# Holding the weights instead of the tokens in the input GEMMs of three FFNs and a convolution mixer

## The chip, the cores and the metric

The kernel runs on one core of a Trainium2 chip. The metric is the device time of one execution in microseconds (us). Three runs of the kernel before gave a median of 1300.48 us, from 1299.72 to 1302.66. The core has five engines that run side by side, each through its own instructions in a fixed order: TensorE (PE, matrix products; its weight loads are listed apart as PEld), VectorE (DVE), ScalarE (ACT), GpSimd (POOL) and SyncE (SP), which here issues all transfers. TensorE multiplies a stationary operand of up to 128 x 128, loaded beforehand, with a moving operand of up to 512 columns and adds the product into a PSUM bank of 128 partitions x 512 fp32 words. There are eight banks. SBUF is the working memory of 128 partitions.

## What is computed

Two layers of a diffusion backbone with 256 latent and 256 context tokens, width 1024, in fp32. Layer 0 is a half-step SwiGLU FFN (latent and context), neighbourhood attention, and a second FFN; layer 1 is an FFN, a gated short convolution, and an FFN. Each sub-layer ends in a residual and a LayerNorm. Cut to what matters:

```
def swiglu_ffn(h, w_in, w_out):                 # w_in (1024, 2*2816), w_out (2816, 1024)
    a, u = jnp.split(h @ w_in, 2, axis=-1)
    return (jax.nn.silu(a) * u) @ w_out

def half_step_ffn(x, shift, scale, gate, w_in, w_out, g, b):
    y = swiglu_ffn(modulate(x, shift, scale), w_in, w_out)      # x * (1 + scale) + shift
    return post_norm_update(x, y, gate, 0.5, g, b)              # layer_norm(alpha*x + 0.5*gate*y)

def short_conv_mixer(h, w_in, conv_w, w_out):   # w_in (1024, 3072)
    b_gate, c_gate, hv = jnp.split(h @ w_in, 3, axis=-1)
    u = c_gate * hv
    y = conv_w[0]*up[:, 0:n] + conv_w[1]*up[:, 1:n+1] + conv_w[2]*up[:, 2:n+2]   # up: u padded by one token
    return (b_gate * y) @ w_out
```

The modulation vectors (shift, scale, gate) are products of a conditioning vector with 18 matrices of 1024 x 1024.

## The kernel before

**Precision.** Every operand of a large product is split exactly into a high part (hi) that the matmul's fast fp32 format holds and the rest (lo); a product is hi*hi + hi*lo + lo*hi, three matmuls. The high part is a ScalarE copy, the low part a VectorE subtraction (`split`, L104 to L106). Weights come by DMA into a raw tile, 256 rows of 512 columns at a time (a *unit*, `wunit` L162), and are split by two ScalarE copies (L178) and two VectorE subtractions (L181). There are 4 raw, 5 hi and 5 lo tiles, and up to three more pairs in some stages, so units are prepared ahead of their use.

**The input GEMMs.** `panels` (L361) goes through the columns of w_in in *panels* of 512: 256 columns of `a` and the matching 256 of `u`. A panel has four units, and there are two tiles of 128 latent tokens, t = 0 and 1. For each (tile, panel, unit), a *chunk*, `mmu` (L152) issues six matmuls with the tokens stationary (128 rows of the width x 128 tokens) and the weights moving (512 columns): L156, L157 for hi*hi and hi*lo, L159 for lo*hi. The first two panels run in an order (`lead_in`) that lets the first token tile start before the second is ready; from the third on, the two tiles alternate unit by unit. A bank holds 128 tokens x 512 columns. When it is full, `done` in `gated` (L380) takes SiLU of its first half on ScalarE (L386) and multiplies by its second half on VectorE (L387). Four chunks later TensorE transposes the result (L395, four transposes of 128 x 128 for both tiles of a panel) into a bank with the 256 columns on the partitions and the tokens along the row, which is then split (L105, L106, named gh and gl): that is the stationary operand of the output GEMM. An FFN has 11 panels. The convolution's input GEMM has 6: two for the gate b, which are transposed by themselves, and four for the products c * hv, which take the same path with a copy in place of SiLU; `conv` then works on the transposed product.

The first FFN of layer 0 is written apart (`f0_mm`, L533): there the weights are stationary and 512 tokens, latent and context, move.

**The tokens.** `modulated` (L324) takes a normalized token tile, transposes it in two halves, applies scale and shift on ScalarE (L341) and splits it into hTh and hTl, tiles of 128 x 512 each, from a pool of 38 such tiles (`act`) that also holds x, the split gated products, gate rows and LayerNorm rows.

**Order.** TensorE's order is the order of the code. The instructions of the other engines are ordered by a planner from modelled times and priorities: `tc.high_priority(offset=n)` moves what it encloses n places ahead. Weights go 40 places ahead, the LayerNorm's and the tokens' work 60 (`LN_EARLY`). The next layer's modulation vectors are made in the background (`ada`, L228): their matrices come by DMA, VectorE sums them up (L242, L244, named acc), and a few matmuls (L260) add over the partitions; a step of it is issued for about every third chunk, 20 places late. PSUM's eight banks are three named mm, three named at and two named tp; token tile 0 uses mm, token tile 1 at, the transposes tp.

Of the kernel before, what the change touches and what calls it, by code (L numbers as in the profile page):

```python
# [28 lines left out]
NACT = 38  # L29
# [35 lines left out]
def backbone_kernel(  # L65
# [28 lines left out]

    def bank(tag, s):
        return pp.tile([P, 512], F32, tag=tag, bufs=PB[tag], name=nm(s))
# [16 lines left out]
    class Late:  # L113
        """work whose TensorE part goes behind n more chunks, or to where its result is first asked for"""
# [37 lines left out]
    def mmu(ps, ops, first, last):  # L152
        """ops: [(lh, ll, rh, rl)] of one unit: hi*hi + hi*lo + lo*hi"""
# [8 lines left out]
    def wunit(srcs, kn, s):  # L162
        """srcs: [(source [P, kn, m], first column)]; returns the exact split (hi, lo), each [P, kn, 512]."""
# [119 lines left out]
    def fold_cols(l, v, m, ln):  # L283
        """column tiles [P, 8] of G = g*(1+scale) and B = b*(1+scale)+shift."""
# [38 lines left out]

    def modulated(z, mv, rs, GB, lag):  # L324
        """z <- norm; -> Late list over halves of (hi, lo) [128 d, 4 chunks, 128 tok] of norm*G + B."""
# [3 lines left out]
        def rest():  # L329
            G, B = GB.get()  # L330
            res = []
            for h in range(2):
# [4 lines left out]
                with tc.high_priority(offset=LN_EARLY):  # L337
                    hi, lo = act(F32R, "hTh"), act(F32R, "hTl")
# [3 lines left out]
                    split(t, hi, lo)  # L342
# [3 lines left out]
        return Late(lag, rest)  # L346

    def hsl(hT, k):
        hi, lo = hT.get()[k // 4]
        s = (k % 4) * P  # L350
        return hi[:, s:s + P], lo[:, s:s + P]

# [1 line left out]
    def lead_in(np):  # L354
        """(tile, panel, unit): the first tile is ready before the second."""
# [3 lines left out]
        return o + [(t, p, u) for p in range(2, np) for u in r for t in range(2)]  # L359

    def panels(cols, w, hTs, order, done, s):  # L361
# [14 lines left out]
    def run(gen):  # L376
        for _ in gen:
            pass
# [682 lines left out]
```

## Time and profile before

| | |
|---|---|
| median of 3 runs | 1300.48 us (1299.72 to 1302.66) |
| profiled execution, first to last instruction | 1296.6 us |
| granted TensorE clock, mean | 0.995 |
| TensorE busy | 1259.6 us (97%), 5890 matmuls |
| weight loads busy | 1006.5 us (78%), 5890 loads |
| VectorE busy | 956.2 us (74%) |
| ScalarE busy | 588.3 us (45%) |
| DMA | 274.92 MB, mean 212 GB/s |

The profiled execution has no other time than this span; the runs' times, taken without the profiler, lie a few microseconds above it. In the profile L12 is line 12 of the kernel; `w1h<-w1r` is what an instruction writes and reads, by the program's tile names; `128x512` is partitions x elements. Behind the bar of a group stand its busy time in us, the mean of one in ns, and the engine's idle time just before, with what ended it. A row of the timeline is start, duration, engine, line, instruction, and in brackets the idle time before it. Matmuls overlap: a row's duration is from a matmul's start to its modelled end, and the time that one takes of TensorE is the distance to the next one's start. Stages by their matmuls: first FFN and attention to 612 us; second FFN's input GEMM 612 to 744 and output GEMM to 809; third FFN's 811 to 939 and to 1003; convolution's input GEMM 1003 to 1074 and output to 1099; fourth FFN's 1100 to 1228 and to 1289.

### The profile page before, as it was taken

How to read it: one execution, taken by the hardware profiler on the slowest of the kernel's cores; microseconds unless marked ns; L12 is line 12 of the kernel's file. 1: busy time of each engine (PE TensorE's matmuls, PEld its weight loads, DVE VectorE, ACT ScalarE, POOL GpSimd, SP SyncE). 2: the span in 40 equal slices, each digit the busy share in tenths (PEclk: the TensorE clock that was granted, in tenths of full speed). 3: DMA queues.
4: the chain of work that ended last, by engine and by line, in shares of the span. 5: the costliest groups of instructions: out<-in, count | busy, mean ns of one | idle time of the engine just before them, and what ended most of it. 6: DMA issues, size and time to landing. Idle time of an engine off the chain costs nothing.

```text
span 1296.6 us, 17135 instructions
## 1 busy us (share of the span) xinstructions
PE 1259.6 (97%) x5890; PEld 1006.5 (78%) x5890; DVE 956.2 (74%) x1691; ACT 588.3 (45%) x1148; POOL 14.4 (1%) x37
## 2 busy tenths in 40 slices
PE   7999989999999999998999999999999999999997
PEld 4787767878778878766787787787788877788886
DVE  3698678686648867788997888767878788865545
ACT  2433013331324556587654534654535644655431
POOL 0000000000001000000000000000000000000000
PEclk9999989999999999999999999999999999999999
DMA  9877578867431632353997988666887664675641
GB/s 283 283 238 237 158 228 277 262 217 246 150 130 53 205 125 74 106 155 101 313 330 257 322 326 302 212 211 209 294 300 255 204 220 148 205 225 179 219 163 57
DMA packets 200305, 274.92 MB, mean 212 GB/s; under 512 B 21196, under 2 KB 145588, under 8 KB 200218
## 3 DMA queue, kind: packets, MB, share of 16 engines
q1 hardware_dynamic: 200218, 273.83, 64.7%
q8 instruction: 46, 0.75, 0.2%
q14 instruction: 41, 0.34, 0.1%
HBM read 269.77 MB, written 4.01 MB: 211 GB/s over the span
## 4 chain that ended last, share of the span: by engine, by line
PE 73%; DMA 12%; DVE 7%; ACT 3%; issue 2%; SPq 1%; POOL 0%; DVEq 0%; ACTq 0%
PE w L156 12%; PE w L157 12%; PE w L159 12%; PE f L538 6%; PE f L539 6%; PE f L540 5%; DMA ar<-in_ada_w_dram 4%; DMA braw<-in_na_rpb_dram 4%; DMA w1r<-in_ffn_w_in_dram 4%; PE wkv L156 2%; PE wkv L157 2%; PE wkv L159 2%; DVE w1l L181 2%; DVE acc L244 2%; PE wc L156 2%
## 5 line engine op out<-in xcount | busy, mean ns | idle before, releaser
L178 ACT ACTIVATE w1h<-w1r 128x512 fp32r<-128x512 f32 x352 | 202.4, 626 | 210.9 <-DMA w1r<-in_ffn_w_in_dram 105.0
L181 DVE TENSOR_TENSOR w1l<-w1r,w1h 128x512 fp32r<-128x512 f32 x352 | 227.3, 686 | 60.4 <-ACT w1h L178 58.0
L156 PE MATMUL w<-w1h,hTh 128*128 128x512 f32 x528 | 210.8, 399 | 4.0 <-ACT hTh L105 4.0
L244 DVE SCALAR_TENSOR_TENSOR acc<-ar,cst,acc 128x512 f32<-128x512 f32 x266 | 187.9, 747 | 34.6 <-DMA ar<-in_ada_w_dram 34.4
L157 PE MATMUL w<-w1l,hTh 128*128 128x512 f32 x528 | 207.0, 392 | 0.0
L156 PE MATMUL w<-w2h,gh 128*128 128x512 f32 (+1 forms) x446 | 175.4, 394 | 0.0
L157 PE MATMUL w<-w2l,gh 128*128 128x512 f32 (+1 forms) x446 | 173.5, 390 | 1.0 <-DVE w2l L181 1.0
L178 ACT ACTIVATE w2h<-w2r 128x512 fp32r<-128x512 f32 x176 | 101.5, 624 | 144.4 <-PE w L159 126.0
L159 PE MATMUL w<-w1h,hTl 128*128 128x512 f32 x528 | 163.4, 391 | 0.6 <-DVE hTl L106 0.6
L181 DVE TENSOR_TENSOR w2l<-w2r,w2h 128x512 fp32r<-128x512 f32 x176 | 113.9, 686 | 44.6 <-ACT w2h L178 44.0
L539 PE MATMUL f<-h0h,w1l 128*128 128x512 f32 x352 | 139.2, 395 | 4.6 <-DVE w1l L181 4.6
L538 PE MATMUL f<-h0h,w1h 128*128 128x512 f32 x352 | 140.5, 399 | 0.0
L540 PE MATMUL f<-h0l,w1h 128*128 128x512 f32 x352 | 139.0, 395 | 0.0
L159 PE MATMUL w<-w2h,gl 128*128 128x512 f32 (+1 forms) x446 | 136.5, 387 | 0.0
L156 PEld LDWEIGHTS w<-w1h,hTh 128*128 128x128 f32 x528 | 99.2, 188 | 28.0 <-ACT hTh L105 5.3
L159 PEld LDWEIGHTS w<-w1h,hTl 128*128 128x128 f32 x528 | 99.0, 188 | 23.9 <-DVE hTl L106 1.5
L157 PEld LDWEIGHTS w<-w1l,hTh 128*128 128x128 f32 x528 | 99.2, 188 | 20.4 <-DVE w1l L181 0.3
L156 PEld LDWEIGHTS w<-w2h,gh 128*128 128x128 f32 x446 | 83.7, 188 | 21.7 <-issue 1.7
L157 PEld LDWEIGHTS w<-w2l,gh 128*128 128x128 f32 x446 | 83.7, 188 | 18.8 <-DVE w2l L181 1.4
L159 PEld LDWEIGHTS w<-w2h,gl 128*128 128x128 f32 x446 | 83.3, 188 | 19.0 <-DVE gl L106 0.3
L539 PEld LDWEIGHTS f<-h0h,w1l 128*128 128x128 f32 x352 | 67.1, 191 | 19.0 <-DVE w1l L181 5.0
L538 PEld LDWEIGHTS f<-h0h,w1h 128*128 128x128 f32 x352 | 66.9, 190 | 18.0 <-issue 4.1
(176 smaller groups left out, 1677.7 us busy)
## 6 DMA issues: line engine op xcount, KB each, us to landing
w1r<-in_ffn_w_in_dram SPq DMA_DIRECT2D x352, 256.0 KB
ar<-in_ada_w_dram SPq DMA_DIRECT2D x128, 512.0 KB
w2r<-in_ffn_w_out_dram SPq DMA_DIRECT2D x88, 512.0 KB
ar<-in_ada_w_dram SPq DMA_DIRECT2D x32, 256.0 KB
wkvr<-in_na_w_qkv_dram SPq DMA_DIRECT2D x32, 256.0 KB
wcr<-in_sc_w_in_dram SPq DMA_DIRECT2D x32, 256.0 KB
wqr<-in_na_w_qkv_dram SPq DMA_DIRECT2D x8, 512.0 KB
bias<-bscr SPq DMA_DIRECT2D x64, 64.0 KB
```

The costliest lines, as they stand in the source:

```text
L156: nc.tensor.matmul(ps, lh, rh, start=first and i == 0, stop=False)
L157: nc.tensor.matmul(ps, lh, rl, start=False, stop=False)
L159: nc.tensor.matmul(ps, ll, rh, start=False, stop=last and i == n - 1)
L178: nc.scalar.activation(hi[:, a:a + m // W_HI], raw[:, a:a + m // W_HI], AF.Copy)
L181: nc.vector.tensor_tensor(out=lo[:, a:b], in0=raw[:, a:b], in1=hi[:, a:b].bitcast(F32), op=ALU.subtract)
L244: nc.vector.scalar_tensor_tensor(out=a, in0=src, scalar=sc, in1=a, op0=ALU.mult, op1=ALU.add)
L538: nc.tensor.matmul(ps, lh, hT0[k][0], start=(k == 0), stop=False)
L539: nc.tensor.matmul(ps, ll, hT0[k][0], start=False, stop=False)
L540: nc.tensor.matmul(ps, lh, hT0[k][1], start=False, stop=(k == KC - 1))
```

## The change

From the third panel on, the input GEMMs of the second, third and fourth FFN and the four product panels of the convolution hold the weights and move the tokens. For this the modulated latent tokens are written into two tiles `hx` of 128 x 4 x 512, one for each half of the width: for each of four 128-row chunks, the hi parts of all 256 tokens and beside them the lo parts. `modulated` writes its hi and lo there instead of into tiles of the pool, which has 30 tiles in place of 38; the two `hx` tiles take as many bytes as the eight left out. (The first FFN's tokens, and those of the attention, use `hx` too, with the same instructions as before.)

A panel is now worked unit by unit for both token tiles at once. For each of two column blocks j of 128 and for z = a, u, `direct_unit` loads 128 x 128 of the hi weights and moves hi and lo of the tokens side by side (512 columns into a whole bank), then loads the lo weights and moves the hi tokens (256 columns into the bank's first half). In the panel's last unit the lo weights come first. A panel fills four banks at a time, two mm and two at, each with 128 columns of the weights on the partitions; the two halves of a bank have still to be added. When a column block's two banks are full, `direct` copies the second half out on ScalarE, adds the first half on VectorE, for a and for u, and then takes SiLU (ScalarE) and the product (VectorE). After the second column block the result is split as before. There are no transposes, since the columns stand on the partitions already, and no delay of four chunks. All of it is issued 60 places ahead. The number of steps between which background work is issued is the same.

```
-NACT = 38
+NACT = 30
+    def hx_tile():
+        return ap.tile([P, 4, 512], F32R, tag="hx", bufs=2, name=nm("hx"))
...
-                    hi, lo = act(F32R, "hTh"), act(F32R, "hTl")
+                    if hx is None:
+                        hi, lo = (act(F32R, n).rearrange("p (k c) -> p k c", k=4) for n in ("hTh", "hTl"))
+                    else:
+                        if len(hx) <= h:
+                            hx.append(hx_tile())
+                        hi, lo = (hx[h][:, :, v * 256 + c0:v * 256 + c0 + P] for v in range(2))
...
-        return o + [(t, p, u) for p in range(2, np) for u in r for t in range(2)]
+        return o + [(None, p, u) for p in range(2, np) for u in r]
...
+    def direct_unit(banks, unit, u, hTs):
+        hi, lo = unit
+        hx = hTs[0].hx
+        for t in range(2):
+            hTs[t].get()
+        for j in range(2):
+            for z in range(2):
+                ps = banks[2 * j + z]
+                c = slice(z * 256 + j * P, z * 256 + (j + 1) * P)
+                for i in range(UK):
+                    k = UK * u + i
+                    h = hx[k // 4][:, k % 4]
+                    last = u == KU - 1
+                    for part in ((1, 0) if last else (0, 1)):
+                        w, m = ((hi, 512), (lo, 256))[part]
+                        nc.tensor.matmul(ps[:, 0:m], w[:, i, c], h[:, 0:m], start=(u == i == part == 0),
+                                         stop=(last and i == UK - 1 and part == 0))
+            yield j
...
+            if t is None:
+                if u == 0:
+                    banks[p] = [mmb(s, z) for _ in range(2) for z in range(2)]
+                for j in direct_unit(banks[p], units[p, u], u, hTs):
+                    if u == KU - 1:
+                        direct(p, j, *banks[p][2 * j:2 * j + 2])
+                    yield
+                    tick()
+                continue
...
+        def direct(p, j, a, u):
+            if j == 0:
+                gs[p] = sp.tile([P, 512], F32, tag="s2", bufs=S2, name=nm("sil"))
+            g = gs[p][:, j * 256:(j + 1) * 256]
+            with tc.high_priority(offset=LN_EARLY):
+                t = sp.tile([P, 512], F32, tag="tmp", bufs=3, name=nm("au"))
+                for z, bk in enumerate((a, u)):
+                    c = slice(z * 256, (z + 1) * 256)
+                    nc.scalar.activation(t[:, c], bk[:, 256:512], AF.Copy)
+                    nc.vector.tensor_tensor(out=t[:, c], in0=bk[:, 0:256], in1=t[:, c], op=ALU.add)
+                nc.scalar.activation(g, t[:, 0:256], func)
+                nc.vector.tensor_tensor(out=g, in0=g, in1=t[:, 256:512], op=ALU.mult)
+                if j == 1:
+                    res.append(finish(p, gs.pop(p)))
...
-            hi, lo = act(F32R, "h0h"), act(F32R, "h0l")
+            hi, lo = (z[:, k] for z in hx0) if k < 4 else (act(F32R, "h0h"), act(F32R, "h0l"))
...
-                hTs[t] = modulated(xt[t], mv, rs, GB[t // 2], F0_LAG[t])
+                hTs[t] = modulated(xt[t], mv, rs, GB[t // 2], F0_LAG[t], hx1 if t < 2 else None, t % 2 * P)
```

More of the change, by code (lines that the diff above doesn't have):

```diff
@@ L322, in finish_stats, with modulated @@
         return mv, rs
-    def modulated(z, mv, rs, GB, lag):
+    def modulated(z, mv, rs, GB, lag, hx=None, c0=0):
         for h in range(2):
@@ L341, in rest @@
                         nc.scalar.activation(t[:, s], ps[:, s], AF.Identity, bias=B[:, c], scale=G[:, c])
-                    split(t, hi, lo)
+                    split(t.rearrange("p (k c) -> p k c", k=4), hi, lo)
                 res.append((hi, lo))
             return res
-        return Late(lag, rest)
+        late = Late(lag, rest)
+        late.hx = hx
+        return late
     def hsl(hT, k):
         hi, lo = hT.get()[k // 4]
-        s = (k % 4) * P
-        return hi[:, s:s + P], lo[:, s:s + P]
+        return hi[:, k % 4], lo[:, k % 4]
     def lead_in(np):
@@ L358, in lead_in, with panels @@
         o += [(t, 1, u) for u in r[2:] for t in range(2)]
-        return o + [(t, p, u) for p in range(2, np) for u in r for t in range(2)]
-    def panels(cols, w, hTs, order, done, s):
+        return o + [(None, p, u) for p in range(2, np) for u in r]
[17 more added lines that the diff above has]
+            yield j
+    def panels(cols, w, hTs, order, done, direct, s):
         units, banks = {}, {}
@@ L397, in done @@
                 res.append(Late(G_LAG, rest))
-        return done, res
+        gs = {}
+        def direct(p, j, a, u):
[12 more added lines that the diff above has]
+                    res.append(finish(p, gs.pop(p)))
+        return done, direct, res
     def order_skew(nu):
@@ L460, in backbone_kernel @@
     hT0 = []
+    hx0 = [hx_tile() for _ in range(2)]
     nar = [0]
@@ L665, in evac @@
                 if nxt:
-                    hTs[t] = modulated(xt[t], mv, rs, GB, (LN_LAG if nk > KC else LT_LAG)[t])
+                    hTs[t] = modulated(xt[t], mv, rs, GB, (LN_LAG if nk > KC else LT_LAG)[t], hx, t * P)
                 else:
@@ L690, in finish @@
             return hi, lo
-        done, gT = gated(AF.Silu, finish, "gT")
+        done, direct, gT = gated(AF.Silu, finish, "gT")
         def done2(p, t, bk):
@@ L697, in done2 @@
                 later()
-        run(panels([(p * 256, FF + p * 256) for p in range(NP)], ffn_w_in[l, j], hTs, lead_in(NP), done2, "w1"))
+        run(panels([(p * 256, FF + p * 256) for p in range(NP)], ffn_w_in[l, j], hTs, lead_in(NP), done2, direct, "w1"))
         drain()
@@ L1000, in backbone_kernel @@
     cols = [(0, 256), (512, 768)] + [(D + n * 256, 2 * D + n * 256) for n in range(4)]
-    run(panels(cols, w, hTs, lead_in(6), done, "wc"))
+    run(panels(cols, w, hTs, lead_in(6), done, cdirect, "wc"))
     drain()
```

5 lines of the change are left out of this document (3 added, 2 removed).

## The prediction

> **What bounds the kernel now.** I read the page first, then the busy times stage by stage, then single panels in the timeline, then the waits of the one stage that looked different. The page:
>
> ```profile
> span 1296.6 us, 17135 instructions
> PE 1259.6 (97%) x5890; PEld 1006.5 (78%) x5890; DVE 956.2 (74%) x1691; ACT 588.3 (45%) x1148; POOL 14.4 (1%) x37
> PE 73%; DMA 12%; DVE 7%; ACT 3%; issue 2%; SPq 1%; POOL 0%; DVEq 0%; ACTq 0%
> ```
>
> TensorE carries 73% of the chain that ended last. The four stages that the change touches are the input GEMMs of the second, third and fourth FFN and of the convolution (window, its length, then busy time of each engine, clock, DMA share):
>
> ```profile
> 612.20:744.40 132.20, 129.70 (x586) 103.36 (x587) 114.90 (x198) 71.62 (x141) 1.07 (x2) 1.00 0.91 305
> 810.90:939.20 128.30, 128.14 (x586) 103.83 (x588) 96.39 (x163) 70.50 (x136) 1.07 (x2) 1.00 0.71 230
> 1002.70:1074.40 71.70, 71.70 (x331) 58.01 (x330) 56.93 (x102) 42.00 (x82) 1.07 (x2) 1.00 0.66 212
> 1100.10:1227.80 127.70, 127.70 (x581) 104.29 (x582) 83.78 (x141) 69.53 (x134) 1.07 (x2) 1.00 0.63 204
> ```
>
> In the last three TensorE has no idle time worth naming, at the full granted clock (1.00). The first, which I call FFN2, is 3.9 us longer than FFN3 for the same products: its VectorE is busy 114.9 of 132.2 us and its DMA engines 0.91 of the time. So a saving on TensorE counts fully in FFN3, FFN4 and the convolution, and in FFN2 only if VectorE, ScalarE and the weights keep up.
>
> **TensorE, per panel.** Before, a panel (256 columns of a and of u) has 48 matmuls of 512 columns and 4 transposes. One panel of FFN4, by the SiLU that follows the same token tile's bank in two panels, and the transposes inside it:
>
> ```profile
> 1157.87 0.38 ACT L386 ACTIVATE sil<-w 128x256 f32<-128x256 f32 x1 [0.21 <-PE w L159]
> 1158.38 0.41 DVE L387 TENSOR_TENSOR sil<-sil,w 128x256 f32<-128x256 f32 x1
> 1163.12 0.60 PE L395 MATMUL gT<-ident,sil 128*128 128x128 f32 x4
> 1163.47 0.48 PE L156 MATMUL w<-w1h,hTh 128*128 128x512 f32 x1
> 1163.78 0.40 PE L157 MATMUL w<-w1l,hTh 128*128 128x512 f32 x1
> 1169.29 0.38 ACT L386 ACTIVATE sil<-w 128x256 f32<-128x256 f32 x1 [0.24 <-PE w L159]
> ```
>
> The panel takes 1169.29 - 1157.87 = 11.42 us. From the first transpose to the second matmul after them are 0.66 us, of which one matmul step, 0.23, would be there anyway: the transposes cost 0.43 us a panel, and 48 matmuls then take 0.229 each.
>
> After the change a unit (256 rows of the weights) gives 8 matmuls of 512 columns (hi weights, tokens' hi and lo) and 8 of 256 (lo weights, tokens' hi): 32 + 32 a panel. The columns streamed are the same, 24,576, but there are 64 weight loads in place of 52. Both prices stand in the trace. The first FFN already holds the weights and moves 512 tokens, and the attention's value products and the last bank move 256 columns with a load each:
>
> ```profile
> 239.97 0.40 PE L540 MATMUL f<-h0l,w1h 128*128 128x512 f32 x1
> ...
> 243.16 0.39 PE L539 MATMUL f<-h0h,w1l 128*128 128x512 f32 x1
> 598.41 0.28 PE L851 MATMUL o<-pT,v 128*128 128x256 f32 x1
> ...
> 599.25 0.40 PE L156 MATMUL wo<-woh,oT 128*128 128x512 f32 x1
> 1284.67 0.28 PE L156 MATMUL w<-w2h,gh 128*128 128x256 f32 x1
> ...
> 1285.38 0.28 PE L156 MATMUL w<-w2h,gh 128*128 128x256 f32 x1
> L850 PEld LDWEIGHTS o<-pT,v 128*128 128x128 f32 x64 | 12.1, 189 | 2.4 <-DVE osum L857 1.1 <-ACT pT L105 0.9
> ```
>
> Fourteen steps in 3.19 us are 0.228 each; seven in 0.84 and six in 0.71 are 0.120 and 0.118, so 0.119 for a short one. A load lasts 0.189 us in its row and still doesn't hold up a step of 0.119: it is hidden, and pipelined with the next. A panel then takes 32 x 0.228 + 32 x 0.119 = 11.10 us, **0.32 less**. Short and long in turn stand nowhere in the trace. Bounds: a short step at half a long one, 0.114, gives 10.94 (saves 0.48); 0.230 and 0.120 give 11.20 (saves 0.22). I take 0.32, from the rows of the same shapes. Panels changed: 9 in each of three FFNs and 4 in the convolution, 31: **-9.9 us** (-6.8 to -14.9), being -2.9 for each FFN and -1.3 for the convolution.
>
> [...]
>
> **VectorE and ScalarE, per panel.** The rows that price it:
>
> ```profile
> L387 DVE TENSOR_TENSOR sil<-sil,w 128x256 f32<-128x256 f32 x66 | 27.0, 417 | 13.6 <-ACT sil L386 13.6
> L386 ACT ACTIVATE sil<-w 128x256 f32<-128x256 f32 x66 | 24.6, 381 | 32.8 <-PE w L159 32.8
> L106 DVE TENSOR_TENSOR gl<-gT,gh 128x512 fp32r<-128x512 f32 x33 | 22.7, 687 | 8.2 <-ACT gh L105 8.1
> L105 ACT ACTIVATE gh<-gT 128x512 fp32r<-128x512 f32 x33 | 19.5, 591 | 24.6 <-PE gT L395 24.6
> ```
>
> Before: two products and a split, 2 x 0.417 + 0.687 = 1.52 us on VectorE; two SiLUs and a copy, 1.35 on ScalarE. After: for each of two column blocks, two copies out of PSUM, two adds, a SiLU and a product: 6 x 0.417 + 0.687 = 3.19 on VectorE (**+1.67**), 6 x 0.381 + 0.591 = 2.88 on ScalarE (+1.53). In FFN3 that makes 96.4 + 15.0 = 111.4 of 125 us, in FFN4 98.8, in the convolution 56.9 + 6.7 = 63.6 of 70: hidden behind TensorE. Since the engines run in order and the new chain passes between them four times, I charge 0.3 us to FFN3 and 0.4 to the convolution (bounds: 0, and 1.67 for each of their 13 panels if nothing hid it). In FFN2 it makes 129.9 of 132.2. Some of what VectorE does there can wait:
>
> ```profile
> 682.28 1.41 DVE L244 SCALAR_TENSOR_TENSOR acc<-ar,cst,acc 128x512 f32<-128x512 f32 x2
> 697.58 1.06 PE L260 MATMUL ada<-acc,ones 128*32 128x512 f32 x8
> 648.00:660.00 12.00, 12.00 (x56) 9.84 (x55) 12.00 (x22) 5.54 (x12) 0.00 (x0) 1.00 0.89 304
> 684.00:696.00 12.00, 12.00 (x56) 9.87 (x55) 7.26 (x14) 5.61 (x12) 0.00 (x0) 1.00 0.63 195
> ```
>
> The modulation sums end at 683.7 and TensorE asks for them at 697.6: 13.9 us of slack. In the crowded 636 to 684 us the change adds 48 / 11.4 x 1.67 = 7.0 us to a VectorE that is at times busy 12.00 of 12; if the sums give way, nothing is late; if the weight splits do, up to 7.0. I take **+1**, since the new chain and the splits are issued ahead of the sums.
>
> **The new wait.** A panel now takes 4 of the 6 banks. So the first unit of the next panel, in its second column block, writes the bank that the last unit's first block has just left: 5 blocks later, each 2 x (0.228 + 0.119) = 0.69, which is 3.47 us, less 0.16 that a matmul's end lies behind the next start. ScalarE's copy and VectorE's add must both be done within **3.3 us**, or TensorE stops with all that is queued on it. In FFN4 copy and product end 0.92 us after the SiLU starts (1157.87 to 1158.79), and the second bank's some 0.4 later: far inside. In FFN2 both engines were late, and two transposes waited for it:
>
> ```profile
> 646.95 0.62 PE L159 MATMUL w<-w1h,hTl 128*128 128x512 f32 x2
> 649.67 0.41 DVE L387 TENSOR_TENSOR sil<-sil,w 128x256 f32<-128x256 f32 x1
> 692.88 0.62 PE L159 MATMUL w<-w1h,hTl 128*128 128x512 f32 x2
> 699.89 0.75 DVE L387 TENSOR_TENSOR sil<-sil,w 128x256 f32<-128x256 f32 x2
> 711.47 0.61 PE L159 MATMUL w<-w1h,hTl 128*128 128x512 f32 x2
> 712.68 0.44 PE L395 MATMUL gT<-ident,sil 128*128 128x128 f32 x2 [0.59 <-DVE sil L387]
> 714.20 0.44 PE L395 MATMUL gT<-ident,sil 128*128 128x128 f32 x2 [1.08 <-DVE sil L387]
> ACT w1h L178 <- DMA w1r<-in_ffn_w_in_dram: 41.8, 23, 5.6
> DVE w1l L181 <- ACT w1h L178: 8.1, 7, 4.5
> ```
>
> The bank that ended at 647.57 was read by 650.08 (2.5 us); the one that ended at 693.50 only by some 700.3 (6.8). ScalarE stood in line behind a weight copy whose transfer was late (41.8 us in 23 waits, longest 5.6). Behind the two matmuls of 711.47 the transposes could have started at 711.93 and gone on at 712.90; they did at 712.68 and 714.20. These 0.75 + 1.30 = 2.1 us go with the transposes: **-2.1**. In their place comes the bank wait: 0 if all nine panels answer like the first, 9 x (6.8 - 3.3) = 31 if all like the second. The new copies are issued ahead of the weight copies, so I lean to the first row: one of nine meets the longest wait, 5.6 + 1.3 - 3.3 = 3.6, and on average half of it is over: **+2**.
>
> **No cost.** The modulated tokens move into two shared tiles that replace 8 of the 38 small buffers; same bytes, same instructions. Only the last output GEMM then holds 4 + 22 + 2 + 4 = 32 tiles against 30, so two LayerNorm rows load later; they are read at the very end. No transfer is added.
>
> **The sum.** FFN2 -2.9 - 2.1 + 1 + 2 = -2.0; FFN3 -2.9 + 0.3 = -2.6; convolution -1.3 + 0.4 = -0.9; FFN4 -2.9: **-8.4 us**. The profiled span of 1296.6 becomes 1288.2; the runs' median lies 3.9 above that span (1300.5), so 1292.
>
> **The rivals.** (1) *The banks are handed over too late in FFN2*, the slower side. At the mean of the two responses, 4.65, and 0.8 for the added copy and add, each of nine panels waits 2.15: +19.4 in place of +2 and +1, so +14.4 - 6.4 = +8, 1308. It decides from a mean wait of 1.3 us (9 x 1.3 eats 5.0 + 6.4). For it: 41.8 us of ScalarE waits; against: the new copies' priority. (2) *VectorE becomes FFN2's bound*: 129.9 busy plus the 8.1 it must wait for ScalarE make 138.0 in place of 130.2: 1300. For it: 12.00 of 12; against: the sums can move. (3) *The short matmuls can't hide their loads* and take 0.189: 31 x (32 x 0.070 - 0.32) = +60, 1360; the rows at 0.119 speak against it. [...] (4) *All hides and a short step takes half a long one*: -14.9 - 2.1 = -17, 1283.
>
> **How the numbers follow.** Forecast 0.55, rival 1 0.18 (0.07 of it within 0.2%, at half its price), rival 2 0.13, rival 3 0.04, rival 4 0.10. A measurement of this kernel can tell 0.2%, 2.6 us, from no change. Faster: 0.55 + 0.10 = 0.65; same 0.07 + 0.13 = 0.20; slower 0.11 + 0.04 = 0.15. Range 1285 to 1305: it holds rival 2, half of rival 1 and part of rival 4, and leaves out under 0.2; the forecast alone spans 1287 to 1297.
>
> **What would show it.** FFN4's panel should take 11.1 us, its short steps 0.119; if they take 0.19, rival 3. A TensorE wait for the VectorE add at a panel's first unit in FFN2 is rival 1; weight products there that wait for the lo split while VectorE is busy throughout are rival 2. FFN4 not shorter by 2 us or more would make the prediction wrong at its root.

## The result: 0.7% slower, and the profile after

| | before | after |
|---|---|---|
| median, runs side by side | 1301.57 us (4 runs, 1299.72 to 1303.87) | 1309.35 us (4 runs, 1308.94 to 1311.71) |
| ratio, 95% interval | | 1.0067 [1.0051, 1.0083] |
| profiled execution | 1296.6 us | 1309.9 us |

The change makes the kernel **slower by 0.67%**; 1292 was predicted, with 1305 as the upper end. The two profiles differ by more, 13.3 us, than the medians, 7.8: in the changed kernel an execution's time is its span and 1.8 us, and by that the profile of before belongs to an execution of about 1298.4, some 3 us faster than its median, while that of the changed kernel (1311.71 us) is the slowest of its four. Stages of single profiles are therefore compared here only where they differ by several us; the verdicts rest on the medians and their intervals.

The page of the changed kernel:

```profile
span 1309.9 us, 18211 instructions
PE 1261.4 (96%) x6262; PEld 1023.7 (78%) x6262; DVE 993.1 (76%) x1815; ACT 625.5 (48%) x1272; POOL 14.8 (1%) x37
PE 67%; DMA 15%; DVE 10%; ACT 3%; issue 2%; SPq 2%; POOL 0%; DVEq 0%; ACTq 0%
```

TensorE has as many us of work as before (1259.6), though a panel has less; its part of the chain that ended last fell from 73% to 67%, and transfers and VectorE took over. The windows of the changed kernel, in the order FFN2's input GEMM, FFN2's output GEMM, FFN3's input GEMM, convolution, FFN4 (window, length, busy time of each engine, clock, DMA share):

```profile
613.90:754.80 140.90, 132.96 (x698) 111.35 (x700) 124.48 (x228) 79.84 (x172) 1.08 (x2) 0.96 0.89 284
755.70:821.60 65.90, 62.32 (x275) 50.26 (x273) 55.97 (x96) 28.62 (x55) 1.07 (x2) 1.00 0.88 302
821.60:955.80 134.20, 129.23 (x698) 109.09 (x700) 106.30 (x196) 80.62 (x171) 1.07 (x2) 0.99 0.73 232
1018.70:1090.10 71.40, 71.40 (x383) 60.13 (x383) 59.85 (x116) 46.84 (x97) 1.07 (x2) 1.00 0.67 209
1115.00:1241.60 126.60, 126.60 (x693) 108.29 (x694) 94.16 (x176) 79.67 (x170) 1.07 (x2) 1.00 0.66 204
```

The convolution and FFN4 are shorter by 0.3 and 1.1 us, with TensorE busy throughout. FFN2 went from 132.2 to 140.9 and FFN3 from 128.3 to 134.2, and there TensorE stands idle for 7.9 and 5.0 us and ran at a granted clock below 1. The waits of FFN2's input GEMM (engine, line, what it waited for, us in all, times, longest):

```profile
ACT w1h L181 <- DMA w1r<-in_ffn_w_in_dram: 37.9, 24, 7.8
PE w L388 <- DVE au L451: 7.2, 4, 3.8
DVE au L451 <- ACT au L450: 6.4, 8, 1.9
```

L388 is the new matmul, L450 and L451 the new copy and sum. The chain behind the longest wait can be followed in the timeline: first VectorE, then ScalarE, then TensorE.

```profile
657.80 1.41 DVE L247 SCALAR_TENSOR_TENSOR acc<-ar,cst,acc 128x512 f32<-128x512 f32 x2
659.12 1.29 DVE L184 TENSOR_TENSOR w1l<-w1r,w1h 128x512 fp32r<-128x512 f32 x2
660.33 0.88 DVE L245 TENSOR_SCALAR acc<-ar,cst 128x512 f32<-128x512 f32 x2
661.12 1.29 DVE L184 TENSOR_TENSOR w1l<-w1r,w1h 128x512 fp32r<-128x512 f32 x2
666.17 0.69 DVE L184 TENSOR_TENSOR w1l<-w1r,w1h 128x512 fp32r<-128x512 f32 x1 [3.76 <-ACT w1h L181]
666.96 0.42 DVE L451 TENSOR_TENSOR au<-w,au 128x256 f32<-128x256 f32 x1
```

```profile
665.51 1.15 ACT L181 ACTIVATE w1h<-w1r 128x512 fp32r<-128x512 f32 x2 [7.83 <-DMA w1r<-in_ffn_w_in_dram]
666.56 0.36 ACT L450 ACTIVATE au<-w 128x256 f32<-128x256 f32 x1
```

```profile
663.40 0.28 PE L388 MATMUL w<-hx,w1l 128*128 128x256 f32 x1
667.44 0.50 PE L388 MATMUL w<-hx,w1h 128*128 128x512 f32 x1 [3.76 <-DVE au L451]
...
669.75 0.79 PE L388 MATMUL w<-hx,w1h 128*128 128x512 f32 x1 [1.35 <-DVE au L451]
670.34 0.41 PE L388 MATMUL w<-hx,w1l 128*128 128x256 f32 x1
...
675.46 0.39 PE L388 MATMUL w<-hx,w1l 128*128 128x256 f32 x1
```

VectorE has worked off splits and modulation sums (acc) one behind the other up to 662.4, and then waits itself. ScalarE stands 7.83 us at a transfer of weights, and the copy out of a full bank (666.56) stands behind it in ScalarE's order, VectorE's sum (666.96) behind that, and TensorE (667.44) behind the sum. The transfer was late, but not because it was issued late. These are the rows of SyncE just before, with two loads of the modulation's bias (adab) ahead of the weights:

```profile
652.51 1.17 SPq L253 DMA_DIRECT2D adab<-in_ada_b_dram  x2
655.14 0.89 SPq L178 DMA_DIRECT2D w1r<-in_ffn_w_in_dram  x2
```

The trace reports the landing of a weight transfer in 16 parts. Of the two transfers issued at 655.14 and 655.55, for which the copy at 665.51 waits, 14 parts had landed by 658.4 and 659.3. The last two parts of each came only by 664.7 and 665.4, behind the bias loads, whose last parts landed at 660.2 and 664.2. The kernel before has the same pair of loads, at 677.22 and 677.84, and ScalarE's longest wait there, the 5.6 us that end at 689.95, is for weights issued right behind them; TensorE does not wait then. The wait at 743 us stands in part behind a third bias load (732.05).

After the second wait the steps go at half speed, at a granted clock of 0.50: from 670.34 to 675.46 lie eight pairs of a long and a short step, 0.64 us each and not 0.35, which costs another 2.3 us. The account of FFN2's input GEMM: 9 panels shorter by 0.18, -1.6 (the panel is measured below); the transposes' waits gone, -2.1; waits at the banks, +7.2; half clock after them, about +4 with that at 743 us: +7.5 of the 8.7 found.

FFN3 loses at its start, where the tokens' LayerNorm stands behind splits and sums on VectorE, and where weights come late behind two more bias loads (issued at 810.58 and 812.18). The waits from 755.7 to 834:

```profile
PE hT L339 <- DVE x L331: 5.2, 2, 3.1
PEld w L159 <- ACT hx L108: 3.0, 2, 2.0
```

### The profile page after: what moved, and what is told of

Its sections match the earlier page's. It is cut to its first block, busy times and chain, and to the rows that moved or that the text cites. A ratio compares the mean times of both kernels' runs of the same rounds, so it can differ in the third digit from the quotient of the medians.

```text
span 1309.9 us, 18211 instructions
## 1 busy us (share of the span) xinstructions
PE 1261.4 (96%) x6262; PEld 1023.7 (78%) x6262; DVE 993.1 (76%) x1815; ACT 625.5 (48%) x1272; POOL 14.8 (1%) x37
## 3 DMA queue, kind: packets, MB, share of 16 engines
q1 hardware_dynamic: 200218, 273.83, 65.6%
## 4 chain that ended last, share of the span: by engine, by line
PE 67%; DMA 15%; DVE 10%; ACT 3%; issue 2%; SPq 2%; POOL 0%; DVEq 0%; ACTq 0%
PE w L388 16%; PE w L159 7%; PE w L160 7%; PE w L162 7%; DMA w1r<-in_ffn_w_in_dram 5%; PE f L597 4%; PE f L599 4%; PE f L598 4%; DMA braw<-in_na_rpb_dram 4%; PE wc L388 3%; DMA ar<-in_ada_w_dram 3%; DVE w1l L184 3%; DVE acc L247 3%; PE wkv L159 2%; PE wkv L160 2%
## 5 line engine op out<-in xcount | busy, mean ns | idle before, releaser
L388 PE MATMUL w<-hx,w1h 128*128 128x512 f32 x864 | 308.0, 402 | 7.7 <-DVE au L451 7.7
L388 PE MATMUL w<-hx,w1l 128*128 128x256 f32 x864 | 239.9, 283 | 0.0
L388 PEld LDWEIGHTS w<-hx,w1h 128*128 128x128 f32 x864 | 162.6, 190 | 48.9 <-DVE au L451 9.3
L388 PEld LDWEIGHTS w<-hx,w1l 128*128 128x128 f32 x864 | 164.9, 191 | 2.5
L598 PE MATMUL f<-h0h,w1l 128*128 128x512 f32 x176 | 69.4, 395 | 3.2 <-DVE w1l L184 3.2
L597 PE MATMUL f<-hx,w1h 128*128 128x512 f32 x176 | 70.0, 398 | 0.0
L597 PE MATMUL f<-h0h,w1h 128*128 128x512 f32 x176 | 69.9, 397 | 0.0
L599 PE MATMUL f<-h0l,w1h 128*128 128x512 f32 x176 | 69.6, 395 | 0.0
L599 PE MATMUL f<-hx,w1h 128*128 128x512 f32 x176 | 69.0, 392 | 0.0
L598 PE MATMUL f<-hx,w1l 128*128 128x512 f32 x176 | 69.0, 392 | 0.0
L108 ACT ACTIVATE gh<-sil 128x512 fp32r<-128x512 f32 x49 | 30.7, 626 | 64.5 <-DVE sil L604 60.6
```

The lines of the kernel that those rows point to most:

```text
L108: nc.scalar.activation(hi, src, AF.Copy)
L388: nc.tensor.matmul(ps[:, 0:m], w[:, i, c], h[:, 0:m], start=(u == i == part == 0), stop=(last and i == UK - 1 and part == 0))
L597: nc.tensor.matmul(ps, lh, hT0[k][0], start=(k == 0), stop=False)
L598: nc.tensor.matmul(ps, ll, hT0[k][0], start=False, stop=False)
L599: nc.tensor.matmul(ps, lh, hT0[k][1], start=False, stop=(k == KC - 1))
```

## The experiments

Lengths are in us from the first matmul of a stage to the first of the next, in the profiled executions; "ratio" is that of the runs to those of before on the same chip, with its 95% interval.

| kernel | median | ratio | FFN2 in | FFN2 out | FFN3 in |
|---|---|---|---|---|---|
| before | 1301.57 | | 133.2 | 65.6 | 129.2 |
| after | 1309.35 | 1.0067 [1.0051, 1.0083] | 141.7 | 66.0 | 135.0 |
| late | 1296.42 | 0.9951 [0.9933, 0.9969] | 132.4 | 64.8 | 128.1 |
| half | 1306.29 | 1.0035 [1.0016, 1.0054] | 135.0 | 72.9 | 128.3 |
| lean_before | 1298.18 | 0.9967 [0.9953, 0.9982] | 134.1 | 62.5 | 128.8 |
| lean_after | 1304.63 | 1.0022 [1.0006, 1.0037] | 132.6 | 74.0 | 129.5 |
| acc256 | 1307.35 | 1.0043 [1.0027, 1.0059] | 130.8 | 75.7 | 129.4 |
| acc256_no3 | 1293.20 | 0.9928 [0.9903, 0.9953] | 130.8 | 62.0 | 129.0 |
| nosum_before | 1302.89 | 0.9996 [0.9981, 1.0010] | 136.2 | 62.8 | 128.7 |
| nosum_after | 1294.73 | 0.9936 [0.9910, 0.9962] | 133.6 | 62.0 | 127.7 |
| pool | 1311.56 | 1.0061 [1.0041, 1.0082] | 137.3 | 67.7 | 129.6 |
| load_before | 1313.42 | 1.0073 [1.0046, 1.0100] | 148.8 | 63.8 | 129.4 |
| spread_before | 1307.13 | 1.0024 [1.0008, 1.0040] | 135.2 | 64.2 | 128.8 |
| spread_after | 1304.10 | 1.0012 [0.9994, 1.0030] | 138.3 | 62.1 | 129.1 |
| late_again | 1296.71 | 0.9940 [0.9919, 0.9960] | 132.8 | 66.8 | 128.7 |
| late_group | 1296.54 | 0.9937 [0.9913, 0.9962] | 134.2 | 65.3 | 128.3 |

### Where it is lost: without FFN2

Theory A, formed on the two traces, was that late transfers of weights hold up the copies out of the banks, and with them a panel's four banks. `late` leaves FFN2 as it was.

```
-        return o + [(None, p, u) for p in range(2, np) for u in r]
+        if not new:
+            return o + [(t, p, u) for p in range(2, np) for u in r for t in range(2)]
+        return o + [(None, p, u) for p in range(2, np) for u in r]
...
-    run(panels(..., hTs, lead_in(NP), done2, direct, "w1"))
+    run(panels(..., hTs, lead_in(NP, (l, j) != (0, 1)), done2, direct, "w1"))
```

> The change is made in FFN3, the convolution and FFN4 alone; FFN2 keeps the old path. Theory A (in FFN2 the evacuation of a bank stands on ScalarE and VectorE behind weight copies whose transfer is late, and TensorE waits for the bank): FFN2's input GEMM is back at 132 us (141 with the whole change), and if the 5.8 us that FFN3's input GEMM lost are a consequence of FFN2's delays, they go too: 1297 to 1299. Theory B (VectorE is the bound wherever it carries 1.67 us more a panel): FFN3 keeps its loss, 1303 to 1305.

The windows of FFN2's input and output GEMM and FFN3's input GEMM in this version:

```profile
615.40:747.00 131.60, 129.28 (x586) 103.46 (x588) 115.16 (x198) 72.10 (x142) 1.07 (x2) 1.00 0.93 308
747.90:812.60 64.70, 62.81 (x279) 50.67 (x277) 53.45 (x89) 25.92 (x49) 1.08 (x2) 1.00 0.91 315
812.70:939.80 127.10, 126.95 (x698) 107.99 (x700) 106.60 (x197) 80.75 (x171) 1.07 (x2) 1.00 0.74 236
```

It is **faster than both kernels**, by 0.49% [0.31, 0.67] against before, somewhat faster than expected. FFN3, which lost 5.9 us in the changed kernel, has no wait left, though its own code is the changed one: it lost for what happened in FFN2. The change in FFN2 alone costs 1.0067 - 0.9951 = 1.2%, about 15 us.

### The bank wait

`half` sends one column block through all four units before the other, so that a panel uses two banks at a time, and there are 11 us until one is asked for again.

```
-        return o + [(None, p, u) for p in range(2, np) for u in r]
+        return o + [(None, p, j, u) for p in range(2, np) for j in range(2) for u in r]
```

> The whole change, but a panel's first column block goes through its four units before the second block starts, so that a panel half holds two banks and a bank has 11 us instead of 3.3 until it is written again. Same matmuls, same evacuation work. Theory A: TensorE's waits for the add (3.8, 1.4 and 1.9 us in FFN2) and the half clock after them vanish, FFN2's input GEMM takes 131 to 133 us, in all 1297 to 1302. Theory B: the same VectorE work takes as long, FFN2 stays at 139 to 141 us and the total at 1307 to 1310.

The windows of its FFN2, input and output GEMM:

```profile
613.70:747.80 134.10, 129.37 (x698) 107.77 (x700) 122.37 (x226) 80.90 (x171) 1.07 (x2) 1.00 0.89 291
748.70:821.70 73.00, 65.25 (x276) 51.54 (x275) 56.93 (x97) 30.29 (x58) 1.07 (x2) 0.95 0.86 293
```

The waits at the banks are gone; in their place TensorE waits for VectorE's splits of weights, six times, 4.0 us in all. FFN2's input GEMM is 6.8 us shorter, and its output GEMM 6.9 longer than in the changed kernel, though there nothing was changed: 5.5 us of it are one wait for the LayerNorm, which stands on VectorE behind sums that waited for their transfers. About half of the loss is left by the medians. The bank is one place at which a delay is paid, not the only one.

### The transfers

In this pair, of three modulation matrices that FFN2 has in the background only one block in eight is loaded, and VectorE sums that one eight times (so the vectors, and the output, are others): 21 transfers of 0.5 MB less, VectorE's work unchanged.

```
-                w = hp.tile([P, D], F32, tag="ar", bufs=3, name=nm("ar"))
-                sync.dma_start(w, ada_w[l, k * P:(k + 1) * P, m * D:(m + 1) * D])
+                if k == 0 or (l, m) not in ((1, 1), (1, 2), (1, 3)):
+                    w = hp.tile([P, D], F32, tag="ar", bufs=3, name=nm("ar"))
+                    sync.dma_start(w, ada_w[l, k * P:(k + 1) * P, m * D:(m + 1) * D])
```

> The kernel before, leaving out part of the computation: of the modulation matrices summed in FFN2's background (three of layer 1) only the first of eight blocks of rows is loaded, and VectorE sums that block eight times. VectorE's work is the same, 10.5 MB of transfers less. Both theories: FFN2's transfers come in time, its input GEMM takes 126 to 130 us instead of 132, in all 1294 to 1299.

> The changed kernel, leaving out the same part as the run beside it. Theory A: with transfers in time no bank is handed over late, and the changed kernel is 3 to 6 us faster than the kernel before with the same part left out: 1290 to 1295. Theory B: VectorE's work in FFN2 is still 130 us, so it is slower than that kernel by 4 us or more: 1299 or more.

The kernel before gains 0.33% by it, though not in FFN2's input GEMM (134.1 us), where it was expected. In the changed kernel FFN2's input GEMM comes back to 132.6 us, and its output GEMM takes 74.0. Beside its pair the changed kernel still loses 6.4 us: late transfers by themselves, theory A in this form, do not make the whole loss. What brought the input GEMM back is not settled. In both kernels of the pair the bias loads come earlier, at 619 and 623 us in the changed one, before the held weights begin at 638; no run moves these loads alone.

### The sums, left out in both

Here the sums over the same blocks are left out too (so the output is another again):

```
+                    if k and (l, m) in ((1, 1), (1, 2), (1, 3)):
+                        continue
                     for h in range(2):
                         src, a = w[:, h * 512:(h + 1) * 512], acc[i][h]
```

> The kernel before, without VectorE's sums over the last 7 of 8 blocks of each of three modulation matrices in the background of FFN2, and without the loads of those blocks (the output is not the reference's). It frees 31 us of VectorE there. All theories: 1295 to 1299, little else, since TensorE bounds FFN2 in the kernel before.

> The changed kernel with the same sums and loads left out. Theory C: VectorE then has 30 us to spare in FFN2, the added 15 us find room, the waits of TensorE in FFN2 and in its output GEMM go, and this is 3 to 7 us faster than the kernel before with the same left out: 1290 to 1294. Theory E (ScalarE's order is the cause: its copies out of the banks and its copies of FFN3's inputs stand behind weight copies that wait for transfers, whatever VectorE has to do): it stays 3 to 8 us slower than the kernel before with the same left out, as it did with only the loads left out: 1300 or more.

The windows of FFN2's input and output GEMM without the sums in the kernel before, and these and FFN3's input GEMM in the changed one:

```profile
616.90:752.30 135.40, 131.54 (x586) 104.53 (x588) 98.53 (x170) 73.37 (x141) 1.08 (x2) 0.99 0.80 252
753.20:815.90 62.70, 62.70 (x279) 50.69 (x278) 44.74 (x76) 26.49 (x50) 1.08 (x2) 1.00 0.74 245
```

```profile
614.80:747.50 132.70, 128.38 (x698) 107.76 (x700) 109.38 (x204) 83.10 (x176) 1.07 (x2) 1.00 0.81 261
748.40:810.40 62.00, 62.00 (x275) 50.47 (x274) 45.30 (x78) 26.83 (x50) 1.07 (x2) 1.00 0.75 243
810.40:937.30 126.90, 126.83 (x699) 107.97 (x699) 106.37 (x197) 80.45 (x171) 1.07 (x2) 1.00 0.75 238
```

With these sums gone the sign turns: the changed kernel is **8.2 us faster** than its pair (1294.73 against 1302.89; the ratios to before differ by 0.60%). All that is lost in FFN2, FFN2's output GEMM and FFN3 is back, with the full clock. The kernel before gains nothing by leaving them out (1295 to 1299 was expected of it), so it is not the sums that are dear, but that they share VectorE's order with the change. Against the pair before, nothing but the sums is left out in addition, and the bias loads stand within 2 us of where they stood there: the changed kernel goes from 1304.63 to 1294.73 us, the kernel before from 1298.18 to 1302.89. Theory C is borne out in sign, with slightly more than the 3 to 7 us that it gave; theory E, by which ScalarE's order alone did it, falls.

### The elementwise work, put on the kernel before

```
         def done(p, t, bk):
+            if extra[0]:        # in FFN2
+                d = sp.tile([P, 512], F32, tag="tmp", bufs=3, name=nm("au"))
+                for z in range(2):
+                    e = slice(z * 256, (z + 1) * 256)
+                    nc.scalar.activation(d[:, e], bk[:, e], AF.Copy)
+                    nc.vector.tensor_tensor(out=d[:, e], in0=bk[:, e], in1=d[:, e], op=ALU.add)
```

> The kernel before, with the elementwise work that the change adds put on top of its old evacuation, in FFN2 alone and for all 11 panels: for each bank two copies on ScalarE and two sums on VectorE of 128 x 256 that nobody uses (per panel 4 x 0.374 = 1.50 us of ScalarE, 4 x 0.419 = 1.68 us of VectorE; in FFN2 18.4 us of VectorE). TensorE's work is that of before. Theory C (the elementwise work that has no room in FFN2 is the cause by itself): slower than before by 6 to 15 us, 1308 to 1317, with the loss in FFN2's input GEMM, its output GEMM or the lead-in of FFN3. Theory G (the loss comes from how the order that is planned for the changed kernel puts the next stage's sums and the weight splits on VectorE, so that a late transfer holds the splits; added work alone is absorbed): 1300 to 1304.

FFN2's input GEMM in this kernel, its first 22.2 us, and the group of the added sums in the stage:

```profile
613.80:761.80 148.00, 135.00 (x586) 107.02 (x588) 132.59 (x245) 85.52 (x183) 1.07 (x2) 0.95 0.89 288
613.80:636.00 22.20, 15.43 (x58) 11.51 (x59) 19.54 (x36) 14.27 (x30) 1.07 (x2) 0.85 0.93 305
L391 DVE TENSOR_TENSOR au<-w,au 128x256 f32<-128x256 f32 x42 | 16.9, 421 | 7.7 <-ACT au L390 7.6
```

Slower by 0.73% [0.46, 1.00], with TensorE's work as before: 16.9 us of sums and their copies lengthen FFN2's input GEMM by 15.6. Added elementwise work can do that by itself, and theory G's 1300 to 1304 is out. But the equal figure of the whole change, 0.67%, proves little. The change in FFN2 costs about 15 us beside `late`, and this run 9.5. Its load is larger, since panels 1 and 2 have it too, and it loses about half just there: in the first 22.2 us TensorE is busy for 15.4 (21.5 in the kernel before) and the clock is 0.85, which makes some 8 of the 15.6 us, with a wait of 6.4 us for tokens that the changed kernel does not have. For the nine panels that the change touches some 7 us are left.

### The held weights without the elementwise work

`acc256` moves hi and lo of the tokens one after the other into the same 256 columns, so that nothing is left to add, and a and u share a bank.

```
-                    for part in ((1, 0) if last else (0, 1)):
-                        w, m = ((hi, 512), (lo, 256))[part]
-                        nc.tensor.matmul(ps[:, 0:m], w[:, i, c], h[:, 0:m], ...)
+                    for n, (w, v) in enumerate(((hi, 0), (hi, 256), (lo, 0))):
+                        nc.tensor.matmul(ps, w[:, i, c], h[:, v:v + 256], ...)
...
-                for z, bk in enumerate((a, u)):      # copies and sums
-                    ...
-                nc.scalar.activation(g, t[:, 0:256], func)
-                nc.vector.tensor_tensor(out=g, in0=g, in1=t[:, 256:512], op=ALU.mult)
+                nc.scalar.activation(g, bk[:, 0:256], func)
+                nc.vector.tensor_tensor(out=g, in0=g, in1=bk[:, 256:512], op=ALU.mult)
```

> All three products of a split pair (hi by hi, hi by lo, lo by hi) are 256 columns long here and go into the same 256 columns of a bank, so no part has to be copied and added: ScalarE and VectorE have a SiLU and a product per column block, as in the kernel before, and a and u share one bank. It separates the held weights from the added elementwise work. Theory C (the loss comes from the 15 us of work added to VectorE, and to ScalarE, within FFN2, which have no room for it there; wherever the work is pushed, TensorE waits): no loss in FFN2, its span 130 to 132 us, and the whole 1294 to 1299, if a short step takes its 0.118 us after another short one too (96 x 0.118 = 11.33 us a panel, 0.09 less than before, over 31 panels 2.8 us). Theory B (holding the weights is what costs, by weight loads that a short step can't cover): short steps over 0.13 us, over 12.5 us a panel, the whole above 1330. Theory D (the transposes that went away, and the order of work around them, cost it): FFN2's span stays above 136 us and the whole above 1302.

FFN2's input and output GEMM, and VectorE and TensorE in the output GEMM:

```profile
616.40:746.30 129.90, 129.05 (x986) 122.57 (x988) 110.22 (x190) 70.36 (x138) 1.08 (x2) 1.00 0.92 301
747.20:822.90 75.70, 67.39 (x275) 53.04 (x273) 57.39 (x97) 28.18 (x53) 1.07 (x2) 0.93 0.87 291
```

```profile
766.11 1.42 DVE L247 SCALAR_TENSOR_TENSOR acc<-ar,cst,acc 128x512 f32<-128x512 f32 x2 [3.46 <-DMA ar<-in_ada_w_dram]
767.44 1.29 DVE L184 TENSOR_TENSOR w2l<-w2r,w2h 128x512 fp32r<-128x512 f32 x2
768.18 0.80 PE L160 MATMUL w<-w2l,gh 128*128 128x512 f32 x1 [5.00 <-DVE w2l L184]
```

As theory C has it, FFN2's input GEMM loses nothing (129.9 us, against 132.2 before), and with short steps of 0.119 us and no loss there, B and D fall. But the whole stayed slower than before, which C did not expect: in the output GEMM VectorE waits for a block of the next FFN's modulation matrix, and the split that TensorE needs stands behind that sum. These sums belong to FFN3, and the planner has pulled them ahead, 30 of them into this output GEMM (the kernel before has 30 there too, and gets by). `acc256_no3` leaves out FFN3's sums and loads instead of FFN2's (the output is again another):

```
+ as in the pair without sums, for the matrices (1, 4), (1, 5), (1, 6)
```

> The variant that accumulates all three products in the same 256 columns (no copies, no sums of parts), without the last 7 of 8 blocks of FFN3's three modulation matrices and their sums (the output is not the reference's). In that variant these sums ran early, 30 of them in FFN2's output GEMM, where VectorE waited 11.4 us for their transfers with the splits of weights behind it. Theory G: FFN2's output GEMM goes from 75 back to 62 to 64 us, and the whole from 1307.4 to 1293 to 1297. Theory H (the held weights themselves, or something else in FFN2's output GEMM, make it late): it stays above 70 us, the whole above 1302.

Its output GEMM of FFN2:

```profile
743.70:805.80 62.10, 62.10 (x276) 50.59 (x275) 40.54 (x72) 28.98 (x55) 1.07 (x2) 1.00 0.73 233
```

1293.2, and TensorE busy without a gap. So two things hold up TensorE by way of VectorE's order: added elementwise work together with the sums (9.9 us between `lean_after` and `nosum_after`), and sums that wait for their transfer ahead of a weight split (3.46 us there, and 5.00 of TensorE, in `acc256`). Why the same 30 sums do no harm in the kernel before was not settled; its longest wait for such a block in that stage is 2.0 us against 3.5 here.

### Two ways to make room

```
-                nc.vector.tensor_tensor(out=g, in0=g, in1=t[:, 256:512], op=ALU.mult)
+                nc.gpsimd.tensor_tensor(out=g, in0=g, in1=t[:, 256:512], op=ALU.mult)
```

> The changed kernel with one edit: the product of the SiLU and of u, both in SBUF here, runs on GpSimd instead of VectorE (0.83 us a panel less for VectorE, 6.7 us in FFN2). No row shows GpSimd at this size. Theory C: about half of what was added to VectorE is gone, and about half of the loss: 1303 to 1306, less if GpSimd is slow (over 3 us a product it would be late for the output GEMM's splits). Theory E: no gain, 1308 to 1311.

```profile
L453 POOL TENSOR_TENSOR sil<-sil,au 128x256 f32<-128x256 f32 x62 | 53.2, 859 | 401.6 <-ACT sil L452 310.3 <-DVE au L451 50.6 <-ACT au L450 27.3
```

No gain: 1311.56. On GpSimd a product takes 0.859 us instead of 0.419. Theory C's number missed, and theory E's (no gain, 1308 to 1311) nearly holds, though E fell above: taking some 7 us from VectorE in FFN2 was not enough, or the slower answer ate it; the profiled execution (1303.9) was the fastest of its ten and can't tell which. This stays open.

The other way deals the sums out later:

```
-    set_background(stream([(1, 1, 0), (1, 2, 0)], [(1, 3, 0)]), 0.35)      # FFN2
+    set_background(stream([(1, 1, 0), (1, 2, 0)]), 0.35)
-    set_background(stream([(1, 4, 0), (1, 5, 0)], [(1, 6, 0)]), 0.35)      # FFN3
+    set_background(stream([(1, 3, 0), (1, 4, 0)], [(1, 5, 0)]), 0.35)
-    set_background(stream([(1, 7, 0)]), 0.4)                               # convolution
+    set_background(stream([(1, 6, 0), (1, 7, 0)]), 0.5)
```

> The changed kernel with the background of modulation sums dealt out later and nothing left out: FFN2 has two matrices instead of three, FFN3 three (one of them FFN2's former), the convolution two instead of one. 16 sums of 0.745 us, 12 us of VectorE, and 4.2 MB go from FFN2 to later stages, where VectorE is busy 106 of 134 us (FFN3). Theory C: FFN2 is relieved of about as much of VectorE as the change adds (14.9 us), so most of the loss goes: 1296 to 1301; if FFN3 and the convolution lose again, up to 1305. Theory G: between 1300 and 1309, since the next stage's sums still run early in FFN2's output GEMM.

> The kernel before with the same dealing out of the modulation sums. Both theories: 1298 to 1303, within 0.3% of before, because TensorE bounds FFN2 there with waits of a few us in all.

FFN2's input and output GEMM of the changed kernel with it:

```profile
615.20:753.70 138.50, 132.36 (x697) 110.34 (x698) 124.19 (x226) 81.47 (x174) 1.07 (x2) 0.98 0.89 284
753.50:815.80 62.30, 62.30 (x275) 50.55 (x274) 47.27 (x83) 28.47 (x55) 1.08 (x2) 1.00 0.81 277
```

VectorE's work in FFN2's input GEMM did not shrink (124.19 against 124.48): 48 sums stand there instead of 52, since those of the next matrices took the places of most that were moved. The relief came in the output GEMM, 47.27 against 55.97, and there, and at FFN3's start, the loss is gone; in the input GEMM 138.5 us stay. The two bias loads stand at 654.59 and 655.21, ScalarE's wait behind them is 7.65 us, and TensorE's at the bank 3.73. By the ratios the changed kernel gains 0.55%, about 7 us; its 1304.1 lies in the ranges of both theories and does not tell them apart. The kernel before loses 0.24%, about 3 us, which no theory expected: of its profile only FFN3's output GEMM is much longer, 69.1 us instead of 62.5.

### The price of a step, and the best version

```
         for j in range(2):
-            for z in range(2):
-                for i in range(UK):
-                    for part in ((1, 0) if last else (0, 1)):
+            for part in ((1, 0) if last else (0, 1)):
+                for z, i in [(z, i) for z in range(2) for i in range(UK)]:
```

> The version that leaves FFN2 as before and holds the weights in FFN3, the convolution and FFN4, once more, beside the next run. It was 1296.4, 0.9951 of before: 1295 to 1298 expected by every theory.

> The same version with the products of a unit in another order: for each 128-column block four 512-column steps and then four of 256, instead of one long and one short by turns. If the alternation makes the long step 0.235 instead of 0.228 us, only one in four stays dear: a panel's 32 long steps lose about 24 x 0.0065 = 0.16 us, over the 22 panels concerned 3.4 us, and the whole is 1292 to 1294. If the long step costs 0.235 for another reason (the held weights, the hi and lo parts side by side), nothing changes: 1295 to 1298, and the steps in the trace stay at 0.235 and 0.118.

Seven panels of FFN4, from a first matmul to a first matmul: long and short by turns (the changed kernel), in fours (`late_group`), and 96 short ones (`acc256`):

```profile
1151.39:1230.08 78.69, 78.69 (x450) 68.62 (x448) 55.73 (x109) 49.13 (x106) 0.00 (x0) 1.00 0.65 199
```

```profile
1137.76:1216.07 78.31, 78.31 (x450) 68.35 (x449) 58.20 (x110) 51.41 (x107) 0.00 (x0) 1.00 0.66 202
```

```profile
1148.26:1228.36 80.10, 80.10 (x674) 80.10 (x673) 46.79 (x79) 41.35 (x77) 0.00 (x0) 1.00 0.65 197
```

A panel takes 78.69 / 7 = **11.24 us** in the changed kernel, 11.19 in fours, 11.44 with short steps alone. Between the starts of matmuls lie on average 0.234 us behind a long one and 0.118 to 0.119 behind a short one; in fours 0.232 and 0.117. The alternation explains a quarter of the difference to the 0.228 of the first FFN at most; the rest is open. The order in fours gains nothing that the runs can tell (0.9937 and 0.9940), where 1292 to 1294 us stood if the alternation were the cause. `late` came out at 0.9940 [0.9919, 0.9960] the second time: it is faster than before, twice, by 0.3 to 0.8%.

## Why the prediction was wrong, step by step

**What bounds the kernel: right, and not carried through.** TensorE bounds FFN3, FFN4 and the convolution; "in FFN2 only if VectorE, ScalarE and the weights keep up" is what decided.

**TensorE per panel: right sign, size off.** 11.10 us were predicted, 11.24 measured. The short step was right (0.119); the long one was taken from the first FFN at 0.228 and takes 0.234. The saving is 0.18 us a panel and not 0.32, over 31 panels 5.6 and not 9.9: 4.3 us of the error. The bounds given, 10.94 to 11.20, did not hold it. FFN4, which has nothing else in it, shows it clean: 1.1 us instead of 2.9, under the 2 us that the prediction called its root.

**VectorE in FFN2: the step that failed.** "If the sums give way, nothing is late" was the ground for +1. The order on VectorE is fixed beforehand, and the sums did not give way: FFN2's input GEMM has 52 of them in the changed kernel and 50 in the one before, and at 657.80 and 660.33 they stand between splits. The slack of 13.9 us between the last sum and TensorE's use of it was real and could not be spent. Also, I looked at the stage's own 132 us; the stretch without room goes on through the output GEMM (before, VectorE is busy 53.4 of 65.6 us there, and the DMA share is 0.89), and what is pushed out of one arrives in the other. The step from the pair without the loads to the pair without the sums shows what the sums cost: 9.9 us less in the changed kernel, nothing gained in the one before. With 30 us of VectorE freed, the change is worth -8.2 beside its pair. A price of the added work in the changed panels alone no run gives; `load_before`, 9.5 us, loses about half of it in other panels.

**The bank wait: place right, weight wrong.** Four waits occurred, 7.2 us in all, and the half clock after them, some 4 us, was not in the sum: about 11 us where +2 stood, the largest error in FFN2's input GEMM. That the longest came out as predicted (3.8 us, 3.6 predicted) is luck: the 3.6 rests on a transfer that is 5.6 us late, and this one was 7.8 late. What failed here is "The new copies are issued ahead of the weight copies, so I lean to the first row": in ScalarE's row the copy at 666.56 still stands behind a weight copy, and that copy waits for the parts behind the two bias loads. The prediction quotes the same wait of the kernel before (5.6 us) and did not ask what made that transfer late.

**FFN3: +0.3 predicted, some +7.5 found** (134.2 against 128.3 - 1.6 by its panels). Not its own evacuation, as `late` shows, but what FFN2 leaves behind: sums and splits ahead of the LayerNorm, and two bias loads ahead of the first weights. The sum had no term for it.

**Rivals.** Rival 1 (banks handed over too late, 1308) is nearest by its number, and the trace has its wait, but four of 7.2 us in all and not nine of 2.15, and `half` without that wait is still slower than before: it names one place where the loss is paid. Rival 2 (VectorE becomes FFN2's bound, 1300) named the right engine and stopped at the end of FFN2's input GEMM. Rival 3 fell: in `acc256` 673 loads, each 0.192 us in its row (the median), stand in 80.10 us, one every 0.119 us, and TensorE is busy for all of it: they are hidden behind the matmuls. Rival 4 asked for steps shorter than any that were found.

What stays open: why `acc256`'s output GEMM is late with as many early sums as the kernel before, why the long step costs 0.234, and why GpSimd's help did not count. That the bias loads hold up the weights behind them is read from the landings in the traces, and no run leaves these loads out or moves them by themselves; so how the loss divides between them and the sums is open too.

## What to carry to other kernels

Before adding work to an engine with idle time left, look at whether its order is fixed and what stands in it around the work: here background sums that had 13.9 us of slack in the kernel before did not give way, and a delay in FFN2 moved on into the next stage (FFN3's input GEMM at 134.2 us, and at 127.1 in `late`). Price the added work by putting it alone on the old kernel, in the panels that the change touches, and look where in the stage the time is lost. For a transfer that lands late, look at what was issued ahead of it and at its last parts before blaming the engine that frees its buffer. And a change that gains in three stages and loses in one is best taken in three: here 1296.5 us instead of 1301.6 or 1309.4.

## What the runs showed of the hardware

Behind short waits of TensorE the granted clock fell to 0.50, twice, which cost time of its own. Around the waits at 743 and at 669 us of the changed kernel (windows: the wait at 743, the first us behind it, the next 3.4; then the slow stretch at 669):

```profile
740.00:743.00 3.00, 1.16 (x7) 0.76 (x6) 1.54 (x4) 1.69 (x4) 0.00 (x0) 1.00 0.82 246
743.00:744.00 1.00, 0.90 (x5) 0.81 (x6) 0.38 (x2) 0.26 (x1) 0.00 (x0) 0.98 0.95 311
744.00:747.40 3.40, 3.40 (x12) 2.92 (x11) 2.73 (x7) 2.74 (x8) 0.00 (x0) 0.50 0.99 395
668.90:675.70 6.80, 5.95 (x19) 5.08 (x20) 6.43 (x13) 5.42 (x14) 0.00 (x0) 0.50 0.69 223
```

A wait of 1.94 us was followed, one microsecond later, by 3.4 us at a granted clock of 0.50, which cost some 1.5 us more; with waits of 3.76 and 1.35 us it was 6.8 us. It does not always happen: behind a longer wait of the same execution the clock stayed at 1.00 (the row of the wait, then the window behind it).

```profile
817.32 1.06 PE L339 MATMUL hT<-ident,x 128*128 128x128 f32 x8 [3.11 <-DVE x L331]
817.30:822.00 4.70, 4.18 (x22) 3.31 (x23) 4.39 (x8) 3.84 (x10) 0.00 (x0) 1.00 0.98 288
```

So 1.94 us were enough once and 3.11 were not another time: the length of one wait does not decide alone.

The bias loads show a second thing: weights landed late behind small transfers. Behind two loads of 128 KB, 14 of the 16 parts of each of two weight transfers of 256 KB had landed by 658.4 and 659.3 us and the last two only by 664.7 and 665.4, some 6 us later. That the small loads are the cause is read from this order; no run leaves them out.
